# Down-projection of a hybrid decoder layer by Strassen's algorithm: seven half-size products instead of eight

## The chip, the core and the metric

The kernel runs on one core of a Trainium2 chip. The engines in this text are PE (TensorE, the matrix engine, with PEld for its weight loads), DVE (VectorE), ACT (ScalarE), POOL (GpSimd), and SP, the queue that issues most transfers. The metric is device time in microseconds (us), the median of several executions. A profile is one further execution, taken with the hardware profiler; its span runs from the first to the last instruction.

## The reference

One layer of a decoder trunk over 1024 prompt tokens and 8 sequences of 4 sample tokens, D = 1024. A mixing sub-layer comes first; then this one, in which the change lies:

```python
    h = rms_norm(x, g_ffn_pre) * (1 + sc2) + sh2
    up = h @ w_up
    up_c, new_ffn = causal_dwconv(up, past_ffn, ffn_conv_w)
    gate, val = jnp.split(up_c, 2, axis=-1)
    ff = (jax.nn.silu(gate) * val) @ w_down
    x = x + gt2 * rms_norm(ff, g_ffn_post)
```

`w_up` is 1024 x 5632 and `w_down` 2816 x 1024. All data are fp32.

## The kernel before

Every fp32 operand of a large matmul is split into a high part in fp32r (a cast on ACT) and a low part (a subtraction on DVE), and a product is three passes: high x high, low x high, high x low. A matmul takes a 128 x 128 stationary operand and streams 512 columns into one PSUM bank.

The order of the work is written by hand. `at(t, f, ...)` enters a piece of work at a virtual time, and `play()` issues all pieces in order of that time; on PE, DVE and ACT the instructions then stand in this order. SP's transfers are ordered by the compiler's scheduler. The down-projection stands behind `play()`, and there ACT and DVE are ordered by the scheduler too, only PE by the program.

**Up-projection** (`for i in range(FT)`, 22 slots). Slot i makes gate tile i and value tile i of 128 features over all tokens, by Strassen's algorithm over token halves: `prod(i, p)` (L1218) is one of seven products, 12 matmuls into one bank. Even token tiles are one half, odd ones the other. `weights` makes sums of up-weights and splits them; `c11`, `c12`, `c21`, `c22` (`comb`, L1233) add banks into the filter's input, which frees a bank; `taps2` (L1280) is the causal filter on DVE; `silu` is on ACT; and `gated` (L1290) multiplies gate and value on DVE and stores the 512 KB product tile to `ffd` in DRAM (L1293).

**Down-projection** (from L1424). Token tiles go in three groups: tiles 0 to 2, 3 to 5, 6 and 7. For each group all 22 rows of `w_down` (128 x 1024 each) are loaded and split again (`w_down(k)`: L109, L114, L119), and the activations of the group are loaded from `ffd` and split (`ff_split`: L1449, L1452, L927). `proj_k` (L723) then does, for each token tile and row, three passes into two banks, 512 columns each. psD holds four tiles of two banks, so that a group of three can be joined by the first tile of the next. The first two rows of group 0 (`first_ld`, `first_hi`, `first_lo`) are loaded and split during the up-projection. In group 1 the sample tokens are projected by `proj_s` (L727), straight from the fp32 rows. `finish` squares and sums a tile on ACT (L140), takes the power on POOL (L134), scales by the gate and adds x1 on DVE (L1472, L1473), and stores y; the last tile, 7, does so in halves (L1485 to L1534), with the last three rows kept for its end.

## Time and profile before

| | us |
|---|---|
| median of 3 runs | 1091.71 (1090.77 to 1092.13) |
| the profiled execution, its own time | 1090.5 |
| its span | 1088.7 |

| engine | busy us | share of the span |
|---|---|---|
| PE | 1058.2 | 97% |
| PEld | 888.0 | 82% |
| DVE | 773.5 | 71% |
| ACT | 468.8 | 43% |
| POOL | 29.7 | 3% |

The busy time of PE is that of pipelined instructions, so a matmul's row is longer than the time by which it sets back the next one; the distance between two starts is what counts. In a row of a group, "busy us, mean ns | idle before us <-releasers" tells how long the engine stood idle ahead of these instructions and what ended it.

### The profile page before, as it was taken

The page shows a single profiled execution, that of the slowest core. Times are in us where ns is not written, and L with a number is a line of the kernel's source. Part 1 is how long each engine was busy: PE and PEld are TensorE (multiplying, and loading weights), DVE is VectorE, ACT ScalarE, POOL GpSimd, SP SyncE. Part 2 cuts the span into 40 slices and gives each one's busy share as a digit, 9 for nine tenths or more (in the row PEclk, how much of TensorE's full clock was granted, in tenths as well). Part 3 has the DMA queues.
Part 4 walks back from the last instruction along what each step waited for, and adds up shares of the span by engine and source line. Part 5 has one row for each costly group of instructions (what it writes and reads, how often), then busy time and mean ns, then how long its engine had stood idle before and what let it go on. Part 6 is the DMA issues. An engine that isn't in the chain of part 4 may idle for free. (4 is left out here: it accounts for less than half of the span.)

```text
span 1088.7 us, 15560 instructions
## 1 busy us (share of the span) xinstructions
PE 1058.2 (97%) x6226; PEld 888.0 (82%) x6226; DVE 773.5 (71%) x1009; ACT 468.8 (43%) x797; POOL 29.7 (3%) x56
## 2 busy tenths in 40 slices
PE   5999999999999989999999999999999999999997
PEld 4999989996887768888888888888887888777786
DVE  5688898887656878778778778777776545433755
ACT  6321111124757654544544544544544434323543
POOL 3000000001011100000000000000000000000000
PEclk9999999999999999999999999999999999999999
DMA  9776651213413213122122122122125975554881
GB/s 340 256 220 195 194 193 49 61 43 95 160 43 132 88 59 117 58 78 97 58 79 97 58 78 98 58 78 97 59 73 162 327 244 166 186 192 145 283 294 49
DMA packets 54849, 145.82 MB, mean 134 GB/s; under 512 B 16628, under 2 KB 25332, under 8 KB 51704
## 3 DMA queue, kind: packets, MB, share of 16 engines
q1 hardware_dynamic: 53432, 140.49, 39.5%
q10 hardware_dynamic: 1344, 4.33, 1.0%
q8 instruction: 49, 0.80, 0.3%
q14 instruction: 24, 0.20, 0.1%
HBM read 123.55 MB, written 21.24 MB: 133 GB/s over the span
## 5 line engine op out<-in xcount | busy, mean ns | idle before, releaser
L119 DVE TENSOR_TENSOR wlo<-raw,whi 128x1024 fp32r<-128x1024 f32 x82 | 100.3, 1223 | 106.8 <-ACT whi L114 106.7
L114 ACT CAST whi<-raw 128x1024 fp32r<-128x1024 f32 x82 | 86.3, 1053 | 152.1 <-PE psd L723 116.3
L1280 DVE SCALAR_TENSOR_TENSOR facc<-fext,par,facc 128x1072 f32<-128x1072 f32 x88 | 117.2, 1332 | 14.2 <-ACT facc L1273 12.6
L535 DVE SCALAR_TENSOR_TENSOR yb<-cext,par,yb 128x1024 f32<-128x1024 f32 x90 | 111.9, 1279 | 0.8
L723 PE MATMUL psd<-whi,yhi 128*128 128x512 f32 x340 | 105.9, 391 | 0.0
L723 PE MATMUL psd<-wlo,yhi 128*128 128x512 f32 x340 | 105.4, 390 | 0.2 <-DVE ms L132 0.2
L723 PE MATMUL psd<-whi,ylo 128*128 128x512 f32 x340 | 105.3, 389 | 0.0
L279 PE MATMUL psa<-hh,whi 128*128 128x352 f32 x372 | 82.0, 328 | 0.0
L279 PE MATMUL psa<-hh,wlo 128*128 128x352 f32 x372 | 80.2, 323 | 0.0
L279 PE MATMUL psa<-hl,whi 128*128 128x352 f32 x372 | 80.1, 323 | 0.0
L723 PEld LDWEIGHTS psd<-whi,yhi 128*128 128x128 f32 x340 | 63.3, 188 | 15.3 <-issue 1.6
L723 PEld LDWEIGHTS psd<-wlo,yhi 128*128 128x128 f32 x340 | 63.7, 188 | 14.3 <-DVE wlo L119 0.6
L723 PEld LDWEIGHTS psd<-whi,ylo 128*128 128x128 f32 x340 | 63.8, 188 | 13.4
L1218 PE MATMUL psc<-hh,sh 128*128 128x512 f32 x176 | 69.3, 394 | 2.8 <-DVE fext L1233 2.8
L1218 PE MATMUL psb<-hh,sh 128*128 128x512 f32 x176 | 71.3, 405 | 0.0
L1218 PE MATMUL psc<-hl,sh 128*128 128x512 f32 x176 | 69.3, 394 | 1.2 <-DVE hl L927 1.2
L1218 PE MATMUL psc<-hh,sl 128*128 128x512 f32 x176 | 69.0, 392 | 0.0
L1218 PE MATMUL psb<-hh,sl 128*128 128x512 f32 x176 | 68.8, 391 | 0.0
L1218 PE MATMUL psc<-bh,whi 128*128 128x512 f32 x176 | 68.6, 390 | 0.0
L1218 PE MATMUL psc<-bh,wlo 128*128 128x512 f32 x176 | 68.5, 389 | 0.0
L1218 PE MATMUL psb<-hl,sh 128*128 128x512 f32 x176 | 68.5, 389 | 0.0
L1218 PE MATMUL psc<-bl,whi 128*128 128x512 f32 x176 | 68.5, 389 | 0.0
(240 smaller groups left out, 2062.3 us busy)
## 6 DMA issues: line engine op xcount, KB each, us to landing
raw<-in_w_down SPq DMA_DIRECT2D x66, 512.0 KB, 4.5
adaw<-in_ada SPq DMA_DIRECT2D x16, 1024.0 KB, 7.4
raw<-in_w_up SPq DMA_DIRECT2D x22, 512.0 KB, 3.6
rawb<-in_w_up SPq DMA_DIRECT2D x22, 512.0 KB, 3.6
ffd<-facc SPq DMA_DIRECT2D x22, 512.0 KB, 2.6
adaw<-in_adag SPq DMA_DIRECT2D x8, 1024.0 KB, 7.4
ffin<-ffd SPq DMA_DIRECT2D x42, 192.0 KB, 3.5
raw<-in_w_in SPq DMA_DIRECT2D x15, 512.0 KB, 4.2
```

The source lines that it names most:

```text
L114: act.copy(hi, ld[0])
L119: dve.tensor_tensor(out=lo, in0=ld[0], in1=hi.bitcast(F32), op=ALU.subtract)
L279: pe.matmul(ps[:, c, 0:CW], lhsT=wt[:, k, :], rhs=h[:, k, c * CW:(c + 1) * CW], start=(k == 0 and n == 0), stop=(k == KT - 1 and n == 2))
L535: dve.scalar_tensor_tensor(out=y[:, 0:NPR], in0=e[:, k:k + NPR], scalar=par[:, off + k:off + k + 1], in1=y[:, 0:NPR], op0=ALU.mult, op1=AL ...
L723: pe.matmul(ps[c], lhsT=s[:, cs], rhs=w[c], start=(first and n == 0), stop=(last and n == len(passes) - 1))
L1218: pe.matmul(out, lhsT=w[:, ks], rhs=h(k), start=(p in (1, 2, 7) and k == 0 and n == 0), stop=(k == 3 and n == 2), skip_group_check=True)
L1280: dve.scalar_tensor_tensor(out=acc[:, 0:1072], in0=e[:, k:k + 1072], scalar=par[:, wo + k:wo + k + 1], in1=acc[:, 0:1072], op0=ALU.mult, o ...
```

## The change

The product of 1024 tokens x 2816 by 2816 x 1024 is cut in halves along all three dimensions: tokens (even and odd tiles), features (even and odd 128-row blocks) and output columns (0 to 511, 512 to 1023). Seven products, each of 4 token tiles x 11 feature blocks x 512 columns, take the place of eight, in the order 2, 3, 1, 6, 5, 7, 4. A step (`step(n)`) is one feature block of one product: 12 matmuls into four banks.

- **Activation sums.** `gated` keeps an even tile's product in a buffer `g` of the pool `whi`, and `fsum` makes four sums (one after an even tile, three after an odd one). Seven half tiles of 256 KB per pair go to DRAM (`fs`), in place of two full ones.
- **Weights.** `w_down` is loaded once (`ld_row`) and stays on chip. `t_sum` makes four sums in place on DVE, three beside the steps of product 1 and one beside those of product 6.
- **Operands.** For each step `a_ld` loads one activation half tile, and `d_hi` (ACT, two casts) and `d_lo` (DVE, two subtractions) split it and the half row of weights. The first four steps are loaded and split during the up-projection.
- **Banks.** Two sets of four banks, Z and X. Products 2, 3 and 5 use Z; 1, 6, 7 and 4 use X, adding up in it. `keep` (ACT) copies Z out, `fold` (DVE) adds a bank to what has been kept. Even token tiles are finished beside product 7; the last five steps of product 4 go token tile by token tile, and each odd tile is finished as it ends.
- **Sample tokens** are projected beside product 1.
- **Order.** All of it stands in the plan of virtual times, ahead of `play()`, and SP's transfers follow that order too, from the output projection on.

```diff
-    ffd = tc.dram_tile([FT, P, NPR], F32, name="ffd")
+    fs = {p: tc.dram_tile([FT // 2, P, 512], F32, name=f"fs{p}") for p in range(1, 8)}
...
+    def tok(v):
+
+        return v[:, 0:NPR].rearrange("p (t h n) -> p t h n", h=2, n=P)
...
     def gated(i):
         ga, va = U["acc", i, 0], U["acc", i, 1]
-        dve.tensor_tensor(out=ga[:, 0:NPR], in0=ga[:, 0:NPR], in1=va[:, 0:NPR], op=ALU.mult)
+        if i % 2 == 0:
+            U["g"] = stream.tile([P, 1024], F32R, name="whi").bitcast(F32)
+            out = U["g"].rearrange("p (h t n) -> p t h n", h=2, n=P)
+        else:
+            out = tok(ga)
+        dve.tensor_tensor(out=out, in0=tok(ga), in1=tok(va), op=ALU.mult)
         dve.tensor_tensor(out=ffs[:, i].rearrange("p (s t) -> p s t", t=ST), in0=acc_parts(ga)[2],
                           in1=acc_parts(va)[2], op=ALU.mult)
-        sync.dma_start(ffd[i], ga[:, 0:NPR])
+        if i % 2 == 0:
+            sync.dma_start(fs[1][i // 2], U["g"][:, 0:512])
+        else:
+            for p, h in ((2, 0), (4, 1)):
+                sync.dma_start(fs[p][i // 2].rearrange("p (t n) -> p t n", n=P), tok(ga)[:, :, h])
+
+    def fsum(i, p):
+        g, ga, va = U["g"], U["acc", i, 0], U["acc", i, 1]
+        if p == 3:
+            sub_to(four(va[:, 0:512]), tok(ga)[:, :, 0], four(g[:, 0:512]))
+            src = va[:, 0:512]
+        elif p == 7:
+            src = va[:, 0:512]
+            sub_to(src, g[:, 0:512], g[:, 512:1024])
+        elif p == 5:
+            src = g[:, 512:1024]
+            dve.tensor_tensor(out=four(src), in0=four(src), in1=tok(ga)[:, :, 1], op=ALU.add)
+        else:
+            src = g[:, 0:512]
+            sub_to(src, g[:, 512:1024], src)
+        sync.dma_start(fs[p][i // 2], src)

...
+    FS = (6.0, 7.5, 9.0)
...
+        for n, p in enumerate((5, 6, 3) if i % 2 else (7,)):
+            at(tv + FS[n], fsum, i, p)
...
-    def first_ld(k):
-        U["wd", k] = stream.tile([P, 1024], F32, name="raw", bufs=2)
-        sync.dma_start(U["wd", k], a["w_down"][k])
-        U["ff", k] = pools["p3"].tile([P, 512], F32, name="s1", bufs=2)
-        sync.dma_start(U["ff", k][:, 0:384], ffd[k, :, 0:384])
...
-    play()
...
+    HK = FT // 2
+    PRODS = (2, 3, 1, 6, 5, 7, 4)
+    TAIL = 5
+    NP_ = len(PRODS) * HK
+    SD, SS = 2.73, 2.0
...
+    def first_b(j):
+
+        raw = stream.tile([P, 1024], F32, name="raw", bufs=2)
+        for h in range(2):
+            sync.dma_start(raw[:, 512 * h:512 * h + 512], a["w_down"][4 * j + 2 * h + 1][:, 0:512])
+        U["fb", j] = raw
...
+    def open_d():
+        psC_cm.__exit__(None, None, None)
+        psD = ctx.enter_context(tc.tile_pool(name="psD", bufs=6, space=PSUM, reuse_waits="tile"))
+        ps = [psD.tile([P, 512], F32, name="psd") for _ in range(6)]
+        W["x"], W["z"] = ps[1:3] + [psb(), psb()], ps[3:6] + ps[0:1]
+        W["s"] = W["z"][0]
...
+    def ld_row(k, hs=slice(0, D)):
+
+        if ("b", k) not in W:
+            W["b", k] = pools["p4" if k % 2 else "p5"].tile([P, D], F32, name=f"b{k}")
+        sync.dma_start(W["b", k][:, hs], a["w_down"][k][:, hs])
...
+    def t_sum(j, n):
+        e, od = W["b", 2 * j], W["b", 2 * j + 1]
+        e1, e2, o1, o2 = (v[:, 512 * h:512 * h + 512] for v in (e, od) for h in range(2))
+        sub_to(*{1: (e1, e2, e1), 3: (e2, o2, e2), 2: (o2, o2, e1), 4: (o1, o1, o2)}[n])
...
+    def a_ld(n):
+        t = R[n, "raw"] = pools["p4"].tile([P, 512], F32, name="fa", bufs=6)
+        sync.dma_start(t, fs[PRODS[n // HK]][n % HK])
...
+    def d_hi(n):
+        own = (n - 4) % 6 < 3
+        hi = (pools["p4"] if own else stream).tile([P, 1024], F32R, name="whi", **({"bufs": 3} if own else {}))
+        act.copy(hi[:, 0:512], R[n, "raw"])
+        act.copy(hi[:, 512:1024], b_raw(n))
+        R[n, "hi"] = hi
+
+    def d_lo(n):
+        own = (n - 4) % 6 < 3
+        lo, hi = (pools["p4"] if own else stream).tile([P, 1024], F32R, name="wlo", **({"bufs": 3} if own else {})), R[n, "hi"]
+        sub_to(lo[:, 0:512], R[n, "raw"], hi[:, 0:512].bitcast(F32))
+        sub_to(lo[:, 512:1024], b_raw(n), hi[:, 512:1024].bitcast(F32))
+        R[n, "a"] = hi[:, 0:512], lo[:, 0:512]
+        R[n, "b"] = hi[:, 512:1024], lo[:, 512:1024]
+
+    def step(n, pairs=range(4)):
+        p, j = PRODS[n // HK], n % HK
+        (ah, al), (bh, bl) = R[n, "a"], R[n, "b"]
+        first = j == 0 and p in (2, 3, 1, 5)
+        for t in pairs:
+            ps, cs = W["z" if p in (2, 3, 5) else "x"][t], slice(P * t, P * t + P)
+            for m, (s, w) in enumerate(((ah, bh), (al, bh), (ah, bl))):
+                pe.matmul(ps, lhsT=s[:, cs], rhs=w, start=(first and m == 0), stop=(j == HK - 1 and m == 2),
+                          skip_group_check=True)
+
+    def ymix(t, h):
+        return W["y", t][:, 512 * h:512 * h + 512]
+
+    def keep(t, p):
+        act.copy({2: lambda: ymix(t, 0), 3: lambda: ymix(t, 1), 5: lambda: W["q", t]}[p](), W["z"][t])
+
+    def fold(t, p):
+
+        out = {1: lambda: ymix(t, 0), 6: lambda: ymix(t, 1), 5: lambda: ymix(t, 1), 7: lambda: W["q", t]}[p]()
+        dve.tensor_tensor(out=out, in0=W["z" if p == 5 else "x"][t], in1=out, op=ALU.add)
+
+    def smp_rows(j):
+        for k in range(4 * j, min(4 * j + 4, FT)):
+            proj_s(W["s"], ffs[:, k, :], W["b", k], k == 0, k == FT - 1)
...
+    at(b + 0.95, open_d)
+    for n in range(4):
+        at(b + 0.96, step, n)
+    at(b + 0.97, open_4)
+    for n in range(4, NP_):
+        p, j = PRODS[n // HK], n % HK
+        at(max(b + 0.98, TS[n] - 13.0), a_ld, n)
+        if p == 2:
+            at(max(b + 0.98, TS[n] - 12.9), ld_row, 2 * j + 1)
+        if n < NP_ - TAIL:
+            at(TS[n] + 0.3, step, n)
+        first_use = min(TS[n], TS[NP_ - TAIL] + SD / 4 * (n - NP_ + TAIL))
+        lead = 6.0 if n == 4 else 7.0 if n < NP_ - TAIL else 4.5
+        for f, th in ((d_hi, first_use - lead), (d_lo, first_use - lead + 1.4)):
+            for q in (2, 3, 1, 6, 7):
+                if end(q) - 2.3 < th < end(q) + 0.1:
+                    th = end(q) + 0.1 + 0.001 * n
+            at(th, f, n)
+    for t in range(4):
+        for n in range(NP_ - TAIL, NP_):
+            at(TS[NP_ - TAIL] + SD * TAIL * t / 4, step, n, (t,))
+    for j in range(4):
+        at(TS[5 + j], ld_row, 2 * j + 1, slice(512, D))
+        at(TS[11 + j], ld_row, 2 * j + 1, slice(0, 512))
+    at(b + 18.0, open_5)
+    for j in range(HK):
+        at(TS[12] + 1.4 * SD * j, ld_row, 2 * j)
+        ts = TS[2 * HK + j]
+        for m, (n, dt) in enumerate(((1, 2.9), (3, 3.5), (2, 4.2))):
+            at(ts + dt, t_sum, j, n)
+        at(TS[3 * HK + j] - 1.0, t_sum, j, 4)
+    at(TS[3 * HK], gates2)
+    for t in range(4):
+        pt = SD / 4 * (t - 3) + 0.05
+        for p in (2, 3):
+            at(end(p) + pt, keep, t, p)
+        for p in (1, 6, 7):
+            at(end(p) + pt, fold, t, p)
+        at(end(5) + pt, keep, t, 5)
+        at(end(5) + pt + 0.5, fold, t, 5)
+        i = 2 * t
+        src = lambda t=t: W["y", t]
+        at(end(5) - 3.0 + 6.5 * t, x1_load, i)
+        at(end(5) + 3.0 + 6.5 * t, fin_sq, i, src)
+        at(end(5) + 5.0 + 6.5 * t, fin_out, i, src, "G")
+        at(end(7) + 3.0 + 3.5 * t, odd_half, t)
+        te = TS[NP_ - TAIL] + SD * TAIL * (t + 1) / 4
+        at(te - 12.0, x1_load, i + 1)
+        at(te + 0.1, odd_fin, t)
+    te = end(1) + 2.0
+    at(te - 4.0, x1_load, 8)
+    at(te, smp_f)
+    at(te + 2.0, fin_sq, 8, lambda: W["f"])
+    at(te + 8.0, fin_out, 8, lambda: W["f"], "Gs")
...
-    psD = ctx.enter_context(tc.tile_pool(name="psD", bufs=4, space=PSUM, reuse_waits="tile"))
-    pss = {}
...
```

## Rows read from the trace of the kernel before

**Rows 1.** The page's first part: busy us (share of the span), instructions.

```profile
PE 1058.2 (97%) x6226; PEld 888.0 (82%) x6226; DVE 773.5 (71%) x1009; ACT 468.8 (43%) x797; POOL 29.7 (3%) x56
```

**Rows 2.** Windows: us; PE, PEld, DVE, ACT, POOL busy; clock; DMA share; GB/s.

```profile
745.00:766.00 21.00, 21.00 (x122) 17.30 (x121) 16.17 (x23) 10.34 (x20) 0.00 (x0) 1.00 0.23 75
830.00:870.00 40.00, 39.54 (x175) 32.78 (x176) 24.45 (x30) 17.56 (x23) 0.00 (x0) 1.00 0.93 311
870.00:910.00 40.00, 40.00 (x178) 33.14 (x177) 16.34 (x19) 14.66 (x20) 0.00 (x0) 1.00 0.71 229
```

**Rows 3.** Timeline of PE at the border: start, us, operation [idle before <-releaser].

```profile
829.19 0.39 PE L1218 MATMUL psb<-hh,sl 128*128 128x512 f32 x1
830.46 0.70 PE L723 MATMUL psd<-whi,sh 128*128 128x512 f32 x2 [0.88 <-DVE fext L1233]
...
838.71 0.61 PE L723 MATMUL psd<-whi,yhi 128*128 128x512 f32 x2
...
859.56 0.62 PE L723 MATMUL psd<-whi,ylo 128*128 128x512 f32 x2
```

**Rows 4.** Timeline of PE around four sample rows.

```profile
932.57 0.61 PE L723 MATMUL psd<-wlo,yhi 128*128 128x512 f32 x2
933.12 1.93 PE L727 MATMUL psd<-raw,ffs 128*32 128x256 f32 x32
934.98 0.73 PE L723 MATMUL psd<-whi,yhi 128*128 128x512 f32 x2
```

**Rows 5.** Timeline of all engines at the end.

```profile
1082.20 0.39 PE L723 MATMUL psd<-wlo,yhi 128*128 128x512 f32 x1
...
1085.08 1.00 SPq L1534 DMA_DIRECT2D out_y<-pt  x2
```

**Rows 6.** Groups by line: count | busy us, mean ns | idle before.

```profile
L723 PE MATMUL psd<-whi,yhi 128*128 128x512 f32 x340 | 105.9, 391 | 0.0
...
L1182 ACT CAST sh<-s 128x512 fp32r<-128x512 f32 x44 | 27.3, 622 | 2.1 <-DVE s L927 2.1
...
L927 DVE TENSOR_TENSOR s<-s,raw 128x512 f32<-128x512 f32 x22 | 15.1, 684 | 0.0
L1233 DVE TENSOR_TENSOR fext<-psb,snb 128x512 f32<-128x512 f32 x22 | 15.0, 683 | 2.3 <-PE psb L1218 2.3
...
L1223 ACT COPY sna<-psc 128x512 f32<-128x512 f32 x22 | 12.8, 580 | 2.7 <-PE psc L1218 2.7
```

**Rows 7.** Timeline of DVE in a steady slot of the up-projection.

```profile
646.79 0.69 DVE L927 TENSOR_TENSOR sl<-raw,sh 128x512 fp32r<-128x512 f32 x1 [2.23 <-ACT sh L1182]
648.37 0.69 DVE L1233 TENSOR_TENSOR fext<-psc,sna 128x512 f32<-128x512 f32 x1 [0.89 <-PE psc L1218]
...
651.68 0.68 DVE L1233 TENSOR_TENSOR fext<-psb,snb 128x512 f32<-128x512 f32 x1
...
656.43 1.23 DVE L1290 TENSOR_TENSOR facc<-facc 128x1024 f32<-128x1024 f32 x1
```

**Rows 8.** Transfers from 825 to 860 us: rate in 40 slices; KB, us to landing.

```profile
GB/s 0 0 0 0 0 0 201 295 172 220 295 372 415 376 201 417 406 236 112 267 274 387 408 427 398 398 417 407 421 406 376 326 341 371 313 318 279 396 345 236
...
raw<-in_w_down SPq DMA_DIRECT2D x12, 512.0 KB, 6.3
ffin<-ffd SPq DMA_DIRECT2D x12, 192.0 KB, 5.5
```

**Rows 9.** Start of the up-projection: PE's timeline, and the window 386.4 to 389.7.

```profile
384.17 0.47 PE L1218 MATMUL psc<-hh,sh 128*128 128x512 f32 x1 [2.75 <-DVE fext L1233]
...
386.77 0.63 PE L1218 MATMUL psc<-hl,sh 128*128 128x512 f32 x1
...
389.33 0.62 PE L1218 MATMUL psc<-hl,sh 128*128 128x512 f32 x1
...
386.40:389.70 3.30, 3.30 (x9) 2.60 (x8) 2.57 (x3) 0.62 (x2) 0.30 (x2) 0.50 0.00 0
```

More of the change, by code (lines that the diff above doesn't have):

```diff
@@ L1410, in first_lo @@
-    def first_lo(k):
-        wh, yh = U["first", k]
-        wl = stream.tile([P, 1024], F32R, name="wlo")
-        sub_to(wl, U["wd", k], wh.bitcast(F32))
-        yl = pools["p3"].tile([P, 512], F32R, name="sl", bufs=5)
-        sub_to(yl[:, 0:384], U["ff", k][:, 0:384], yh[:, 0:384].bitcast(F32))
-        U["first", k] = k, (yh, yl), [halves(wh), halves(wl), U["wd", k]]
-    for k in range(2):
-        at(b - 14.0 + 5.0 * k, first_ld, k)
-        at(b - 8.0 + 3.0 * k, first_hi, k)
-        at(b - 6.9 + 3.0 * k, first_lo, k)
@@ new lines, in body, with first_b_hi @@
+    HK = FT // 2
[3 more added lines that the diff above has]
+    SD, SS = 2.73, 2.0
+    W, R = {}, {}
+    def first_b(j):
[3 more added lines that the diff above has]
+        U["fb", j] = raw
+    def first_b_hi(j):
+        hi = U["fbh", j] = stream.tile([P, 1024], F32R, name="whi")
+        act.copy(hi, U["fb", j])
@@ new lines, in first_b_lo, with first_a, first_a_hi @@
+    def first_b_lo(j):
+        lo, hi = stream.tile([P, 1024], F32R, name="wlo"), U["fbh", j]
+        sub_to(lo, U["fb", j], hi.bitcast(F32))
+        for h in range(2):
+            R[2 * j + h, "b"] = [t[:, 512 * h:512 * h + 512] for t in (hi, lo)]
+    def first_a(n):
+        raw = U["fa", n] = pools["p3"].tile([P, 512], F32, name="s1", bufs=2)
+        sync.dma_start(raw, fs[2][n])
+    def first_a_hi(n):
+        hi = U["fah", n] = pools["p3"].tile([P, 512], F32R, name="sh", bufs=5)
+        act.copy(hi, U["fa", n])
@@ new lines, in first_a_lo @@
+    def first_a_lo(n):
+        lo = pools["p3"].tile([P, 512], F32R, name="sl", bufs=5)
+        sub_to(lo, U["fa", n], U["fah", n].bitcast(F32))
+        R[n, "a"] = U["fah", n], lo
+    def open_d():
[4 more added lines that the diff above has]
+        W["s"] = W["z"][0]
@@ new lines, in gates2, with x1_load, fin_sq @@
+    def gates2():
+        W["G"] = pools["p5"].tile([P, D], F32, name="G")
+        W["Gs"] = pools["p5"].tile([NS * ST, D], F32, name="Gs")
+        load_gate(W["G"], 1)
+        load_gate_s(W["Gs"], 1)
+    def x1_load(i):
+        xt = W["xt", i] = pools["p5"].tile([P, D], F32, name="px", bufs=3)
+        sync.dma_start(xt[:tile_rows(i)], x1d[i * P:i * P + tile_rows(i), :])
+    def fin_sq(i, src):
+        rows = tile_rows(i)
+        W["r", i] = rstd_of(sq_sum(pools["p5"], src()[:rows], rows), rows, 1.0 / D)
@@ new lines, in fin_out, with smp_f @@
+    def fin_out(i, src, g):
+        rows = tile_rows(i)
+        t, xt = src(), W["xt", i]
+        dve.tensor_tensor(out=t[:rows], in0=t[:rows], in1=W[g][:rows], op=ALU.mult)
+        dve.scalar_tensor_tensor(out=t[:rows], in0=t[:rows], scalar=W["r", i][:rows], in1=xt[:rows], op0=ALU.mult, op1=ALU.add)
+        sync.dma_start(o["y"][i * P:i * P + rows], t[:rows])
+    def smp_f():
+        f = W["f"] = pools["p5"].tile([NS * ST, D], F32, name="pf")
+        for q in range(4):
+            (dve.tensor_copy, act.copy)[q % 2](f[:, 256 * q:256 * q + 256], W["s"][32 * q:32 * q + 32, 0:256])
@@ new lines, in half_sq, with odd_half @@
+    def half_sq(src):
+        junk = pools["p5"].tile([P, D], BF16, name="junk", bufs=1)
+        ss = small.tile([P, 1], F32, name="ss")
+        act.activation(junk[:, 0:512], src, AF.Square, accum_out=ss)
+        return ss
+    def odd_half(t):
+        ss = half_sq(W["q", t])
+        v0 = W["v", t] = pools["p5"].tile([P, 128], F32, name=f"v{t}")[:, 0:1]
+        dve.tensor_scalar(out=v0, in0=ss, scalar1=1.0 / D, scalar2=EPS, op0=ALU.mult, op1=ALU.add)
+        dve.tensor_tensor(out=W["q", t], in0=W["q", t], in1=W["G"][:, 512:1024], op=ALU.mult)
@@ new lines, in body @@
+    TS = {}
+    t = b + 1.0
+    for n in range(NP_):
+        if 2 * HK <= n < 3 * HK and (n - 2 * HK) % 2 == 0:
+            at(t + 0.2, smp_rows, (n - 2 * HK) // 2)
+            t += SS
+        TS[n] = t
+        t += SD
+    TS[NP_] = t
+    end = lambda p: TS[(PRODS.index(p) + 1) * HK - 1] + SD
+    for j, t0 in ((0, b - 16.0), (1, b - 12.0)):
+        at(t0, first_b, j)
+        at(t0 + (6.5 if j == 0 else 7.5), first_b_hi, j)
+        at(t0 + (7.6 if j == 0 else 8.6), first_b_lo, j)
+    for n, (t0, t1) in enumerate(((-15.9, -10.0), (-15.8, -9.0), (-8.0, -3.6), (-7.9, -2.2))):
+        at(b + t0, first_a, n)
+        at(b + t1, first_a_hi, n)
+        at(b + t1 + 0.7, first_a_lo, n)
```

145 lines of the change are left out of this document (34 added, 111 removed).

## Prediction, made before the change was run

> **What bounds the kernel now.** I read the page's engine table first: PE is busy for 97% of the span [rows 1], so a change counts if it takes matmuls away, or opens a gap between them. Then the windows: PE is full in the steady up-projection and in the down-projection, while DVE works 16.17 us of 21.00 in the first, and DMA runs at 311 GB/s just behind the border between them and at 229 GB/s later [rows 2]. Third, PE in order of time. The last up-projection matmul starts at 829.19, the first of the down-projection at 830.46 behind a wait of 0.88 us on the DVE sum that frees the bank, and then they come in pairs: from 838.71 to 859.56 there are 46 pairs in 20.85 us, 0.2266 us for each matmul [rows 3]. (The 390 ns that the groups show as the mean of one is latency; the pitch is what a matmul costs.) Every fourth weight row or so the sample tokens cut in: four rows take from 933.02 (one pair after 932.57) to 934.98, 1.96 us [rows 4]. At the end, the last matmul starts at 1082.20 and what follows is a chain through ACT, DVE and POOL to the last store [rows 5].
>
> So the down-projection holds PE from 829.42 (829.19 and one pitch) to 1082.43, that is 253.0 us. Of it 1056 matmuls (8 tiles x 22 rows x 2 halves x 3 passes; 3 x 340 in the groups [rows 6] and 36 at the start) take 239.3, the 22 sample rows 5.5 x 1.96 = 10.8, and 2.9 us are waits, 1.0 of them at the entrance.
>
> **The change, part by part.**
>
> *Matmuls.* Seven products of 11 row pairs, 4 token tiles and 3 passes are 924 matmuls of the same shape; 132 go. The up-projection's products already run twelve in a row into one bank, at the same pitch (its PE is 21.00 of 21.00 busy [rows 2]), so I take 0.2266: 924 x 0.2266 = 209.4 us. The sample rows stay, 10.8 us. The new stage is 220.2 us plus W, the waits; the old was 253.0.
>
> *Sums in the up-projection.* Per pair of tiles DVE gets four more 128x512 operations, at 0.684 each [rows 6] 2.7 us in two slots, 2.1 of them after an odd tile's product. In a slot DVE stands idle 2.23 us until ACT has cast, and later 0.89 until PE ends a product [rows 7]; it has waited for PE before it comes to the sum that PE needs next (the one at 651.68), so 2.1 us behind the product at 656.43 is absorbed. Cost nothing; without that cover it would be up to 2.1 us in each of 11 slots, 23 us. The gated product itself only writes in another order, and stays at 1.2 us (its row ends where the next begins, at 657.7).
>
> *Stores and loads.* Seven 256 KB stores per pair take the place of two of 512 KB, where the windows show 75 GB/s [rows 2]: hidden. SP follows the written order now, and waits for DVE ahead of each of these stores. What stands behind them are the next up-weights, asked for a slot ahead, and at the border the loads of steps 7 to 9. The written order also holds in the output projection, where x tiles come behind one weight row and the first up-weights behind an x tile; they are wanted by DVE and ACT later, so I take 0, and a late one costs at most its landing, 6.3 us for 512 KB [rows 8]. Three loads of w_down become one, 22 MB less; since those are hidden today, "weights on chip" gains nothing by itself.
>
> *Weight sums and operands.* A step needs four casts' worth of 128x512: two on ACT (2 x 0.622) and two subtractions on DVE (2 x 0.684) [rows 6], 1.24 and 1.37 us beside 2.72 us of PE: hidden. In the third product three weight sums come on top: DVE 5 x 0.684 = 3.4 us per step, where PE has 2.72 and on average 0.98 of sample work, 3.7. Covered, with 0.3 to spare.
>
> *The waits W.* The trace has no Strassen down-projection, so each is bounded.
> (a) Entrance: 0 if the first banks are free (the first three tiles' banks belong to finished products), 1.0 as today [rows 3]. I take 0.3.
> (b) First loads. Steps 4 to 10 each need a 256 KB activation and a 512 KB weight row, 0.79 MB in 2.72 us, 289 GB/s, and nothing of it can start before the up-projection's tiles are free at 829.4. Steps 0 to 3 give 10.9 us of cover. Today's second block is issued at the same place, and loads landed 6.3 us after issue [rows 8]. Then 1.24 on ACT and 1.37 on DVE make it some 9 us; DVE is by then through most of the last tile's sums. Step 7 is the tight one: its buffer is still being stored from, and SP asks for its data only after the last gated product. The steady slot's two filter operations, product and bank sum run from 651.68 to about 657.7 [rows 7], 6 us; with a wait for ACT and one more sum I put SP's request at 9 us: 9 + 6.3 + 2.6 = 17.9 against 19.0. Bounds 0, and 5.0 if the rate fell to the 229 GB/s of the next window (3.43 us a step, 7 x 0.71). I take 0.6, since the same window shows nine slices running between 387 and 427 GB/s [rows 8].
> (c) Bank hand-over between products. Emptying a bank takes 0.58 us on ACT or 0.69 on DVE [rows 6], and PE returns to it 2.05 us after it left. Four in a row at 0.69 against PE's 0.68 fit unless DVE is behind. Bounds 0, and 0.7 at each of four hand-overs, 2.8. I take 0.5.
> (d) The last five steps run tile by tile, so five operand pairs are wanted within 2.7 us: DVE needs 5 x 1.37 = 6.9 us from 3.1 us ahead, so the fifth is 0.8 late; 0 if DVE is early. I take 0.6.
> W is 2.0, between 0 and 9.6.
>
> *The end.* The last tile goes through the same square, mean, power, scale and two half stores [rows 5]: no change.
>
> The sum: the profiled execution has a span of 1088.7 and a time of 1090.5 us. 1090.5 - 253.0 + 220.2 + 2.0 = 1059.7. The median of the runs shown is 1091.71, 1.2 above that execution; I give part of it back and say **1060.0 us**.
>
> **A rule of the Trainium skill against it.** In 825 to 860 us DMA moved 387 to 427 GB/s over nine slices (0.9 us each) with transfers of 192 and 512 KB, several in flight [rows 8]. "DMA: Bandwidth & Descriptors", section Bandwidth, asks for transfers of 1 MiB to reach three quarters of the peak and lists 138 GB/s for 64 KB and 341 for 1 MB; for the change's 256 KB pieces I estimate some 230 GB/s from that page's two figures, and (b) would come to 7 x (0.79 MB / 230 GB/s - 2.72) = 4.8 us. The trace disagrees with it for queued transfers, by the nine slices; what it would do here is rival A.
>
> **Rivals.**
> A. *The first product waits for its loads.* For it: DMA is 93% busy in 830 to 870 today [rows 2], and SP holds the loads of steps 7 to 9 behind DVE's last sums. Against: the slices near 400 GB/s [rows 8]. Time: 1059.7 + 4.4 = 1064.
> B. *DVE becomes the bound of the third product.* Dependent sums do not overlap, and any wait on ACT adds. At 4.1 us a step instead of 3.7 it costs 11 x 0.4 = 4.4: 1064.
> C. *The up-projection's DVE queue slips*, so that a freed bank comes late to PE after every odd tile: up to 11 x 2.1 = 23 us, 1083. Against: 3.1 us of idle in every slot [rows 7], 2.23 + 0.89.
> D. *Slower than before: PE falls to its half clock.* Behind a wait of 2.75 us at 384 and a short one after it, the granted clock was 0.50 from 386.4 to 389.7, the 1.2 GHz level, and matmuls came at 0.427 us (six from 386.77 to 389.33) [rows 9]. Each matmul so run costs 0.200 more; 132 saved ones are worth 29.9 us, so 150 slow matmuls, 13 of the 77 steps, decide. If a third of the stage (308) ran so, it would be +62: 1121. For it: a wait at each of many steps, through operands made one at a time. Against: PE is fed today by the same casts and never leaves 1.00 in the stage [rows 2]. "TensorE: Matmul & The Clock Gate", section "A second HAM failure mode: psum-queue depth-cycling" in the Trainium skill, describes such a clock loss in a kernel that cycles through PSUM banks; this change cycles through four banks in a step, the trace before through three tiles with no loss.
> E. *The change does not do what it says*: as many matmuls as before. Then 1090. The diff counts 924, so this is almost nil.
>
> **How the numbers follow.** Forecast (W up to 4) 0.74, A 0.11, B 0.07, C 0.03, D 0.03, E 0.01, and 0.01 for the rest. Range: from W = 0 (1057.7), less the runs' scatter of 0.7, to W at its upper end of 9.6, 1067, where A and B lie too; it leaves out C, D and E, and a reserve for what I have not thought of. A measurement of this kernel can tell 0.2% (2.2 us) from no change. Faster by more than that: forecast, A, B, C: 0.95; within: 0.02; slower: 0.03.
>
> **What would show it.** Right: 924 matmuls in the stage besides the sample rows at a pitch of 0.227; the span from the last up-projection matmul to the last of all near 222 us; whi and subtractions on DVE waiting for PE or loads, not PE for them; PE in the steady up-projection still 21.00 busy of 21.00. A would show as PE waiting for ACT or DVE, and these for DMA, at 840 to 860; B as PE waiting for DVE subtractions around 890 to 930; C as waits on fext sums in the up-projection; D as a granted clock under 1 in the stage. I am wrong if the stage takes over 230 us, or if the up-projection grows by more than 2.

## The result, and the profile after

The changed kernel takes **1061.92 us**, the median of four executions (1059.50 to 1063.64), against 1091.92 beside it: a ratio of 0.9726, 95% interval 0.9709 to 0.9743. Run again unedited it took 1060.98 (0.9723, interval 0.9710 to 0.9737). Forecast were 1060.0, in 1057 to 1067. The profile shown here is the slowest of the first four: 1063.64, span 1061.8.

The page's first part, as in [rows 1]:

```profile
PE 1030.5 (97%) x6094; PEld 864.8 (81%) x6094; DVE 825.0 (78%) x1142; ACT 466.6 (44%) x835; POOL 38.2 (4%) x56
```

PE has 132 instructions fewer (6226 to 6094) and stays at 97%: the time went with the matmuls, and PE is still the bound. DVE has 133 more and 51.5 us more of work, in a shorter span.

The windows, with the columns of [rows 2]:

```profile
745.00:766.00 21.00, 21.00 (x122) 17.34 (x121) 16.76 (x24) 10.02 (x19) 0.00 (x0) 1.00 0.26 82
830.00:870.00 40.00, 40.00 (x178) 33.14 (x177) 30.05 (x45) 23.46 (x39) 0.00 (x0) 1.00 0.91 336
870.00:910.00 40.00, 40.00 (x247) 30.52 (x246) 21.39 (x35) 16.58 (x30) 0.00 (x0) 1.00 0.52 194
910.00:950.00 40.00, 40.00 (x234) 30.66 (x233) 34.84 (x56) 12.69 (x24) 5.67 (x1) 1.00 0.24 73
950.00:1000.00 50.00, 49.84 (x219) 40.69 (x218) 34.36 (x56) 24.39 (x45) 0.97 (x1) 1.00 0.43 129
1000.00:1040.00 40.00, 40.00 (x178) 33.14 (x177) 36.06 (x59) 22.97 (x46) 4.63 (x4) 1.00 0.63 217
272.00:277.00 5.00, 5.00 (x14) 3.63 (x15) 2.23 (x2) 4.09 (x6) 0.00 (x0) 0.66 0.00 1
```

Six things stand here. PE is full in the steady up-projection although DVE has its sums (16.76 now, 16.17 in [rows 2]). It is full at the border too, where it stood at 39.54 of 40. The clock is 1.00 all through the last stage. DMA carries 336 GB/s in its first 40 us. DVE, at 16 to 24 of 40 us in the old stage, is at 34.84 and 36.06: the next limit. And far ahead of the change, at 272 to 277 us, this execution has a granted clock of 0.66.

PE's timeline at the border, around sample rows, and at the stage's last matmul, as in [rows 3, 4, 5]:

```profile
832.00 0.39 PE L1218 MATMUL psb<-hh,sl 128*128 128x512 f32 x1
832.23 0.39 PE L1532 MATMUL psd<-whi,sh 128*128 128x512 f32 x1
...
914.42 0.39 PE L1532 MATMUL psb<-wlo,whi 128*128 128x512 f32 x1
914.74 1.93 PE L727 MATMUL psd<-b,ffs 128*32 128x256 f32 x32
916.60 0.50 PE L1532 MATMUL psd<-whi 128*128 128x512 f32 x1
...
1053.91 0.39 PE L1532 MATMUL psb<-wlo,whi 128*128 128x512 f32 x1
```

The first matmul of the stage comes one pitch behind the last of the up-projection; the 0.88 us wait of [rows 3] is gone. From 832.23 to 1053.91 are 221.7 us.

I made one table from the first and last starts of the matmul lines in each trace (us). "Middle" runs from the first matmul of the output projection (L833) to the first of the up-projection, "up-projection" from there to the first of the down-projection, "stage" from the first to the last matmul of the down-projection, "end" from there to the end of the span.

| kernel | first L833 | middle | up-projection | stage | end |
|---|---|---|---|---|---|
| before | 256.6 | 112.9 | 461.0 | 251.7 | 6.5 |
| changed | 256.3 | 115.2 | 460.8 | 221.7 | 7.9 |
| changed, again | 257.5 | 113.3 | 460.8 | 221.7 | 6.4 |

The stage gives 30.0 us in both profiles. The wait at its entrance is gone too, but the up-projection as a whole is only 0.2 us shorter for it: from the first to the last of its own matmuls (L1218) it took 459.7 us before and 460.5 in both changed profiles. The granted clock from 381 to 394 us was 0.87 in the first and 0.74 in the other two; `tail_pt` below, a changed kernel with all its sums, has 0.87 there and 459.8. So these 0.8 us go with the execution's clock and not with the sums. The first profile lost 2.3 us in the middle and 1.4 at the end; the second hardly any of either.

### The profile page after: what moved, and what is told of

The parts are those of the page before. It is cut to its first block, busy times and chain, and to the rows that moved or that the text cites. A ratio compares the mean times of both kernels' runs of the same rounds, so it can differ in the third digit from the quotient of the medians.

```text
span 1061.8 us, 15512 instructions
## 1 busy us (share of the span) xinstructions
PE 1030.5 (97%) x6094; PEld 864.8 (81%) x6094; DVE 825.0 (78%) x1142; ACT 466.6 (44%) x835; POOL 38.2 (4%) x56
## 5 line engine op out<-in xcount | busy, mean ns | idle before, releaser
L1532 PE MATMUL psd<-whi 128*128 128x512 f32 x204 | 80.1, 393 | 0.0
L1532 PE MATMUL psd<-whi,wlo 128*128 128x512 f32 x204 | 79.6, 390 | 0.1
L1532 PE MATMUL psd<-wlo,whi 128*128 128x512 f32 x204 | 79.5, 390 | 0.1
L1513 ACT CAST whi<-fa 128x512 fp32r<-128x512 f32 x73 | 45.3, 621 | 70.9 <-PE psb L1532 24.6
L927 DVE TENSOR_TENSOR wlo<-fa,whi 128x512 fp32r<-128x512 f32 x73 | 49.9, 684 | 31.0 <-ACT whi L1513 31.0
L1218 PE MATMUL psc<-hh,sh 128*128 128x512 f32 x176 | 69.7, 396 | 2.8 <-DVE fext L1233 2.8
L1218 PE MATMUL psb<-hh,sh 128*128 128x512 f32 x176 | 71.3, 405 | 0.0
L1218 PE MATMUL psc<-hl,sh 128*128 128x512 f32 x176 | 69.6, 396 | 0.9 <-DVE hl L927 0.9
L1218 PE MATMUL psc<-hh,sl 128*128 128x512 f32 x176 | 69.4, 395 | 0.0
L1218 PE MATMUL psb<-hh,sl 128*128 128x512 f32 x176 | 68.8, 391 | 0.0
L1218 PE MATMUL psc<-bh,whi 128*128 128x512 f32 x176 | 68.6, 390 | 0.0
L1218 PE MATMUL psc<-bh,wlo 128*128 128x512 f32 x176 | 68.5, 389 | 0.0
L1218 PE MATMUL psc<-bl,whi 128*128 128x512 f32 x176 | 68.5, 389 | 0.0
L1218 PE MATMUL psb<-hl,sh 128*128 128x512 f32 x176 | 68.5, 389 | 0.0
L279 PEld LDWEIGHTS psa<-hh,whi 128*128 128x128 f32 x372 | 62.8, 189 | 6.4 <-issue 4.1
L279 PEld LDWEIGHTS psa<-hh,wlo 128*128 128x128 f32 x372 | 63.8, 188 | 0.0
L279 PEld LDWEIGHTS psa<-hl,whi 128*128 128x128 f32 x372 | 63.1, 188 | 0.0
```

The lines of the kernel that those rows point to most:

```text
L279: pe.matmul(ps[:, c, 0:CW], lhsT=wt[:, k, :], rhs=h[:, k, c * CW:(c + 1) * CW], start=(k == 0 and n == 0), stop=(k == KT - 1 and n == 2))
L927: dve.tensor_tensor(out=out, in0=x, in1=y, op=ALU.subtract)
L1218: pe.matmul(out, lhsT=w[:, ks], rhs=h(k), start=(p in (1, 2, 7) and k == 0 and n == 0), stop=(k == 3 and n == 2), skip_group_check=True)
L1513: act.copy(hi[:, 0:512], R[n, "raw"])
L1532: pe.matmul(ps, lhsT=s[:, cs], rhs=w, start=(first and m == 0), stop=(j == HK - 1 and m == 2), skip_group_check=True)
```

## The experiments

**The loss ahead of the stage and the end.** Four kernels ran beside each other. `again` has no edit.

> The changed kernel once more, unedited, beside the three that follow, so that edits worth 1 to 3 us can be read against it. Theory (the profile of the changed kernel shows 1.7 us of slower matmuls after a wait at 272 us, which the other executions may or may not have): 1059.5 to 1063.6 us, as the four executions so far, and in the profile a last stage of 221 to 223 us from the first to the last matmul. Rival (the 2.8 us lost ahead of the stage belong to the change in every execution): the profile again shows the 0.5 clock behind 272 us and 1063 or more.

Measured: 1060.98 us, interval above; the profiled execution has no half clock at 272 us. PE's timeline in the changed kernel (the second row stands for those at half clock):

```profile
271.99 0.86 PE L607 MATMUL psb<-w,pw 128*128 128x352 f32 x2 [2.22 <-DVE yb L454]
...
274.62 1.38 PE L607 MATMUL psb<-w,pw 128*128 128x352 f32 x2
```

The same instruction in `again`, and then the window 272 to 277 us there:

```profile
272.53 0.86 PE L607 MATMUL psb<-w,pw 128*128 128x352 f32 x2 [1.56 <-DVE yb L454]
```

```profile
272.00:277.00 5.00, 4.47 (x19) 3.42 (x19) 2.78 (x3) 3.54 (x4) 0.00 (x0) 1.00 0.03 12
```

The wait is there in both, as before the change (1.8 us there), but only behind the wait of 2.22 us did the matmuls slow down. The eleven other profiles with this wait, the kernel before among them, have it at 1.01 to 1.81 us, a granted clock of 1.00 behind it and a middle of 112.1 to 113.8. So the middle's loss is one of the single execution. It may be part of why the eight executions of this kernel lie between 1059.2 and 1063.6.

`wlo` takes the wait away:

```diff
-    at(11.6, w_lo, 0)
+    at(14.4, w_lo, 0)
-    at(13.7, w_lo, 1)
+    at(14.5, w_lo, 1)
```

> The changed kernel with the two subtractions of w_out rows 0 and 1 moved behind the three multiplications that finish the layer norm (they stand between them on VectorE and wait for a late load there). Theory (the matmul at 272 us waits 2.2 us for a multiplication that stands behind the first subtraction, and the granted clock falls to one half behind the wait): the wait and the half clock both go, 2 to 4 us less than the unedited kernel. Rival 1 (the rows are what is late, and the wait only moves to the first matmul that uses them, at 278 us): 0 to 0.5 us less. Rival 2 (the half clock is not tied to the wait): 2.2 us less, and the half clock stays in 273 to 277 us.

Measured: 1059.22 us (1058.60 to 1062.30), ratio 0.9716, interval 0.9700 to 0.9733. The middle takes 111.4 us, where twelve profiles without this edit, the kernel before among them, have 112.1 to 115.2, and the window has neither wait nor slow matmul:

```profile
272.00:277.00 5.00, 5.00 (x22) 3.84 (x22) 0.23 (x1) 4.99 (x8) 0.00 (x0) 1.00 0.01 2
```

So the stretch is 1.9 us shorter than in `again`; in the whole time the two intervals overlap, and 1.8 us between the medians is not told apart from nothing. Rival 1 falls by the stretch. Rival 2 can't be judged: `again` had no half clock to lose.

`tail_pt` gives the end four buffers:

```diff
-        u = pools["p5"].tile([P, 512], F32, name="pt", bufs=2)
+        u = pools["p5"].tile([P, 512], F32, name="pt", bufs=4)
```

> The changed kernel with four buffers instead of two for the products of the last four odd token tiles with the gate. Theory (tile 5's product waited 2.63 us for a buffer whose store had been issued late, and so tile 5's scalings stood ahead of tile 7's): that wait is gone, from the last matmul to the end of the span 6.3 us as before the change, instead of 7.66, and 1.4 us less in the time than the unedited one. Rival (the end is set by the 5.3 us of vector work itself behind the last matmul): 7.5 us or more, and no difference.

Measured: 1059.22 us (1058.97 to 1062.22), 0.9716, interval 0.9701 to 0.9732, which overlaps that of `again`. DVE's timeline in the changed kernel:

```profile
1053.83 0.69 DVE L1593 TENSOR_TENSOR pt<-psb,G 128x512 f32<-128x512 f32 x1 [2.63 <-DMA out_y<-pt]
...
1056.64 0.15 DVE L1595 SCALAR_TENSOR_TENSOR ms<-ss,v 128x1 f32<-128x1 f32 x1
```

and in `tail_pt`:

```profile
1051.82 0.69 DVE L1593 TENSOR_TENSOR pt<-psb,G 128x512 f32<-128x512 f32 x1 [0.50 <-ACT junk L1579]
...
1055.22 0.16 DVE L1595 SCALAR_TENSOR_TENSOR ms<-ss,v 128x1 f32<-128x1 f32 x1 [0.50 <-ACT junk L1579]
```

Tile 5's product waited 2.63 us for a store to leave its buffer, and the small operation that tile 7 needs next (L1595) stood behind it on DVE until 1056.64, 2.7 us after the last matmul; with four buffers it comes 1.2 us after. The end is 6.4 us here. With two buffers it is 6.4 to 7.9 from run to run (`again`: the wait was 1.08 and the end 6.4), so the theory holds for the mechanism: the wait is gone. Its 1.4 us were the difference of one execution; what the edit is worth on average is not told apart from nothing.

`sp_auto` takes the hand-written order off SP:

```diff
-    with tc.manual_schedule(engines={mybir.EngineType.SP}):
-        play()
+    play()
```

> The changed kernel without its hand-written order for SyncE, whose issues the planner then orders as in the kernel before. Theory (the written order moved loads but none that the wait at 272 us hangs on): the wait at 272 us stays at 1.8 to 2.3 us, and the part ahead of the last stage differs by less than 1 us; in the stage itself the planner's order may bring loads late, which shows as waits of the stage's matmuls. Rival (the written order costs the 2.8 us ahead of the stage): the first matmul of the stage comes 2 to 3 us earlier, at 829.4 us as before.

Measured: **1068.45 us** (1067.26 to 1069.68), 0.9795, interval 0.9781 to 0.9809; 0.7% (7.5 us between the medians) slower than `again`, and all of it in the stage, which takes 229.2 us. The first matmul of the stage comes at 829.83, 2.4 us earlier than in the first profile, which is the sign that the rival named. But `nf_first` and `nf_wait` below keep the written order and have it at 829.85 and 829.71, with a middle of 112.9 and 113.3 (112.8 here). So the 2.4 us go with the execution, and the rival falls. The timeline of `sp_auto` (SP and PE), and then two windows of it:

```profile
829.83 0.39 PE L1532 MATMUL psd<-whi,sh 128*128 128x512 f32 x1
...
836.36 0.34 SPq L1482 DMA_DIRECT2D out_n_f<-fst  x1
...
839.61 0.40 SPq L1508 DMA_DIRECT2D fa<-fs  x1
...
845.67 0.80 PE L1532 MATMUL psd<-whi 128*128 128x512 f32 x1 [4.80 <-ACT whi L1514]
846.26 0.63 PE L1532 MATMUL psd<-whi,wlo 128*128 128x512 f32 x1
846.69 0.63 PE L1532 MATMUL psd<-wlo,whi 128*128 128x512 f32 x1
```

```profile
840.00:845.00 5.00, 0.87 (x4) 0.38 (x2) 0.69 (x1) 0.62 (x1) 0.00 (x0) 0.91 1.05 313
845.00:850.00 5.00, 4.33 (x10) 3.45 (x11) 4.35 (x7) 3.34 (x6) 0.00 (x0) 0.50 1.03 412
```

SP in the changed kernel:

```profile
832.42 0.32 SPq L1508 DMA_DIRECT2D fa<-fs  x1
832.79 0.43 SPq L1494 DMA_DIRECT2D b<-in_w_down  x1
```

This has the signs of rival A: PE waits for ACT at 845.67, and ACT for the loads. But the loads held back are those of step 4 on, not those of steps 7 to 9. The scheduler puts the store of the conv states, which waits for the last filter, and three stores of activations (two of the gated product, one of a sum) ahead of the first loads. These go out 9.8 us after the stage's first matmul (839.61 against 829.83), where the changed kernel has 0.2 (832.42 against 832.23). Step 4 waits 4.8 us, and behind the wait the granted clock is 0.50, the 1.2 GHz level: one matmul comes after 0.59 us and eleven after 0.427 instead of 0.227, another 2.6 us. 4.8 + 2.6 = 7.4 of the 7.5 us that the stage is longer.

**Is it that store?** Two kernels move it to the front by hand.

```diff
+    at(b + 0.975, n_f_out)
```

(`n_f_out` is the store, taken out of `open_5`.)

> The changed kernel with one store moved on SyncE: the 396 KB of conv states go out ahead of the first loads of step 4 instead of 18 us into the stage (the planner's order, without the hand-written one, had put it there). The store waits for the last convolution at about 836 us. Theory (that one store held all first loads back): the loads are issued 7 us later, at 839 to 840 us instead of 832.4, a matmul of step 4 or 5 waits 4 to 5 us at half clock behind it, 1067 to 1069 us, as without the written order. Rival (other loads that the planner moved were what counted): 1060 to 1062 us.

Measured: 1062.82 us (1061.17 to 1063.34), 0.9738, interval 0.9724 to 0.9753, stage 223.3. The expectation's premise was not met: at that place the store stood ahead of the last filter in the program, did not wait for it and went out at 833.68. The loads still came later, and one matmul waited 0.65 us. The timeline of `nf_first` (PE and SP):

```profile
829.85 0.39 PE L1534 MATMUL psd<-whi,sh 128*128 128x512 f32 x1
...
834.07 0.43 SPq L1510 DMA_DIRECT2D fa<-fs  x1
...
849.70 0.50 PE L1534 MATMUL psd<-whi 128*128 128x512 f32 x1 [0.65 <-ACT whi L1516]
```

The next kernel has the store in the place that was meant:

```diff
+    at(tv + 1.72, n_f_out)
-        at(max(b + 0.98, TS[n] - 13.0), a_ld, n)
+        at(max(tv + 1.75, TS[n] - 13.0), a_ld, n)
```

(and the same for `ld_row`.)

> The changed kernel with the store of the conv states put behind the operations that make the last of them, and the first loads of the last stage (steps 4 on) put behind the store; the run before this one had the store too early, so that it went out at 833.7 us, with states of the last tile that were not ready, and held nothing up. Theory (loads that stand behind this store on SyncE come 4.3 us later, at 836.7 instead of 832.4; without the written order they came 7.2 us later, and 4.8 us of that were waited for): a matmul of step 4 or 5 waits 1.5 to 2.5 us and the clock falls behind it, 2 to 5 us more than the changed kernel's 1061. Rival (the loads have so much room that 4 us more are covered): within 0.7 us.

Measured: 1066.27 us (1063.69 to 1067.25), 0.9775, interval 0.9759 to 0.9792, some 0.5% (5.3 us) over `again`; the profiled execution is the fastest of its four (1063.69). The timeline of `nf_wait` (SP and PE):

```profile
829.71 0.39 PE L1534 MATMUL psd<-whi,sh 128*128 128x512 f32 x1
...
836.23 0.34 SPq L1482 DMA_DIRECT2D out_n_f<-fst  x1
836.62 0.42 SPq L1510 DMA_DIRECT2D fa<-fs  x1
...
842.06 0.50 PE L1534 MATMUL psd<-whi 128*128 128x512 f32 x1 [1.31 <-ACT whi L1516]
...
852.07 0.50 PE L1534 MATMUL psd<-whi 128*128 128x512 f32 x1 [1.25 <-ACT whi L1516]
```

The stage takes 225.8, 4.1 more. The waits that the trace names are 1.31, at step 4, and 1.25, at step 7, and the matmuls just behind each come at up to 0.39 us (842.06, 842.39, 842.78) with a granted clock of 1.00 in the window from 840 to 845.

How late the loads are has to be counted in each execution from its own first matmul of the stage; the expectations compared times since the start of different executions, and the stage began up to 2.5 us earlier in some than in others.

| kernel | first matmul of the stage | first load issued | later than in the changed kernel | stage longer by |
|---|---|---|---|---|
| changed | 832.23 | 832.42 | 0 | 0 |
| `nf_first` | 829.85 | 834.07 | 4.0 | 1.6 |
| `nf_wait` | 829.71 | 836.62 | 6.7 | 4.1 |
| `sp_auto` | 829.83 | 839.61 | 9.6 | 7.5 |

So step 4 has some 5 us of room: in the changed kernel its last cast ends 5.0 us ahead of its first matmul, 4.0 us of lateness cost it no wait, 6.7 one of 1.31 and 9.6 one of 4.80. The tight step is 7, as the prediction had it: in `nf_first` its own load was issued only 0.5 us later (10.2 instead of 9.7 us after the stage's first matmul), but behind the late ones, its last cast ended at 19.8 instead of 16.2, and its matmul, due at 19.0, waited. The rival falls, since 4.0 us are not covered in full.

As to the question: the store of the conv states alone makes 4.1 of the 7.5 us. In `sp_auto` the three stores behind it go out from 837.61 on, 7.8 us after the stage's first matmul; in the changed kernel they go out at the same distance (from 840.00), because they wait for DVE's last products. Loads that stand behind these stores would be as late without the store of the conv states; that is argued from the issue times, and no kernel here has those three ahead of the loads without it.

**Does the same line help the kernel before?** `sp_before` has SP in written order there (the same `with` around `play()`).

> The kernel before with the one line of the change that is not Strassen: SyncE in written order up to the last stage. Theory (in the kernel before no matmul waits for a load that this order could bring earlier; the last stage shows 2.9 us of waits in all): within 1.5 us of the kernel before. Rival (the written order is worth the 7.5 us that its removal cost the changed kernel, whatever the algorithm): 1083 to 1086 us.

Measured: 1091.82 us, ratio 1.0005, interval 0.9995 to 1.0014; stage 251.7. The line is worth nothing in the output and the up-projection. It doesn't reach the old stage, which stands behind `play()`, so the run says nothing of the order there. In the changed kernel it guards the entrance of the stage, whose steps 4 to 10 need 0.79 MB each.

**Where the gain is.** `eight` issues the steps of one product twice:

```diff
             at(TS[n] + 0.3, step, n)
+            if p == 6:
+                at(TS[n] + 0.31, step, n)
```

> The changed kernel with every step of the product numbered 6 issued twice, so that the stage has 8 x 132 = 1056 matmuls again; loads, splits and stores stay as they are (that product is counted twice in what it is added to). Theory (the stage is as long as its matmuls, 226.7 ns each): 132 x 0.2267 = 29.9 us more, 251.6 us from the first to the last matmul of the stage, and 1090 to 1092 us, the time of the kernel before. Rival (the gain comes from the weights that stay on chip and from the order of the loads): 1065 to 1075 us.

Measured: 1090.12 us, ratio to the kernel before 0.9993, interval 0.9981 to 1.0005; stage 250.8, that is 29.1 more (forecast were 29.9; the changed kernel has a loss of 0.7 us at 950 us, in product 6, that `eight` hasn't). The groups of `eight` in the stage, and of the changed kernel:

```profile
L1532 PE MATMUL psd<-whi 128*128 128x512 f32 x226 | 88.6, 392 | 0.0
```

```profile
L1532 PE MATMUL psd<-whi 128*128 128x512 f32 x204 | 80.1, 393 | 0.0
```

(This is one of three passes into the banks called psd, 22 more; each pass into those called psb has 22 more too, and 6 x 22 are 132.) With as many matmuls as before, and with single loads, kept weights and SP's order all in place, the gain is gone. `onchip` is the other side, the kernel before with its weights loaded once (the later passes split a constant tile):

```diff
-        ld = split_load(a["w_down"][k], 2)
+        ld = (w0, 2) if g else split_load(a["w_down"][k], 2)
```

> The kernel before with the rows of w_down loaded in the first of its three passes over the tokens only; the other two passes split a constant tile instead, so 44 loads of 512 KB are left out, and the products of those passes are not those of the weights. Theory (weights kept on chip save nothing by themselves, since no matmul of the stage waits for such a load): within 1.5 us of the kernel before. Rival (the traffic slows the stage, and keeping weights is part of the gain): 3 us or more below.

Measured: 1091.14 us, ratio 0.9999, interval 0.9987 to 1.0011. One of its windows:

```profile
870.00:910.00 40.00, 40.00 (x178) 33.15 (x177) 16.93 (x20) 13.94 (x20) 0.00 (x0) 1.00 0.49 163
```

Traffic falls from 229 GB/s [rows 2] to 163 in this window, and PE is busy 40.00 of 40.00 us in both kernels. The rival falls.

**What the added vector work costs.** `nosums` leaves `fsum` its stores but not its sums (`src` is then the unsummed block).

> The changed kernel without the 44 sums of activation blocks in the up-projection (11 + 33 operations of 0.69 us on VectorE, 30 us); the stores stay and carry blocks that are not summed, so four of the seven products work on wrong data. Theory (the sums lie in time that VectorE has free beside the matmuls): no change, within 1.5 us of the changed kernel's 1061. Rival (VectorE's queue slips in the up-projection, as the third rival of the prediction): up to 23 us less.

Measured: 1062.36 us (1060.95 to 1063.09), 0.9735, interval 0.9721 to 0.9750; up-projection 460.7, as with them.

```profile
745.00:766.00 21.00, 21.00 (x122) 17.30 (x122) 15.69 (x22) 10.08 (x19) 0.00 (x0) 1.00 0.26 84
```

DVE has 1.07 us less in this stretch, PE the same 21.00. `dve2` goes the other way in the stage:

```diff
-        sub_to(lo[:, 512:1024], b_raw(n), hi[:, 512:1024].bitcast(F32))
+        for _ in range(2):
+            sub_to(lo[:, 512:1024], b_raw(n), hi[:, 512:1024].bitcast(F32))
```

> The changed kernel with the second of the two subtractions of every step of the last stage issued twice, 73 x 0.684 = 50 us more on VectorE. Theory (VectorE was busy 34.8 of 40 us from 910 to 950 us and 36.1 of 40 us from 1000 to 1040 us, so it has 4 to 5 us of room in each such stretch, in which 14 to 15 steps would now add 10 us): VectorE becomes the bound in those stretches, matmuls wait for it, 5 to 13 us more than the changed kernel. Rival (the splits run so far ahead that the stage carries it, 158 + 50 of 215 us): 2 us more or less.

Measured: **1080.48 us** (1080.41 to 1082.26), 0.9907, interval 0.9892 to 0.9921; 19.5 more than `again`, beyond the theory's 13. The stage takes 239.6. Windows of `dve2`, and then two rows of PE's timeline in it:

```profile
910.00:950.00 40.00, 34.51 (x196) 25.52 (x195) 37.07 (x61) 8.82 (x17) 0.03 (x1) 0.91 0.26 75
950.00:1000.00 50.00, 48.88 (x215) 39.73 (x214) 48.07 (x75) 20.71 (x38) 2.09 (x1) 1.00 0.42 129
1000.00:1040.00 40.00, 35.63 (x153) 28.81 (x152) 35.49 (x53) 19.23 (x36) 4.18 (x4) 0.97 0.41 136
```

```profile
939.16 0.77 PE L1533 MATMUL psd<-whi 128*128 128x512 f32 x1 [5.49 <-DVE ye L1545]
...
1038.62 0.77 PE L1533 MATMUL psd<-whi 128*128 128x512 f32 x1 [3.77 <-DVE yo L1545]
```

DVE falls behind within a product and PE pays where it needs a bank that DVE must empty (`fold`, here L1545): 5.5 us at the end of product 1, 3.8 at the end of product 7, 11.3 of PE's waits in all. Of the 17.9 us by which the stage is longer 6.6 are not waits that the trace names; some 5.6 of them are matmuls that come at 0.427 us behind the two long waits, where the granted clock is 0.57 from 938 to 946 us and again from 1037 to 1045. The rival (the stage as a whole has room) falls: 158 + 50 of 215 us did not fit, because the room is not where the work is.

**A version that beats both?** `best2` joins `tail_pt` and `wlo` and tries one more wait, 2.8 us at the entrance of the up-projection:

```diff
-        for dt, f in ((0, sq1), (2.2, rs), (2.4, gt), (3.7, res), (4.9, sq2), (6.0, rs), (6.8, xn2)):
+        for dt, f in ((0, sq1), (2.2, rs), (2.4, gt), (5.85, res), (5.95, sq2), (7.05, rs), (7.8, xn2)):
-        at(t8 + (6.1 if i == 0 else 14.6), c11, i)
+        at(t8 + (7.86 if i == 0 else 14.6), c11, i)
```

> The changed kernel with three edits of order: the four buffers at the end, the two subtractions of w_out rows behind the layer norm, and, at the entrance of the up-projection (383 to 390 us), the sample tile's sum and one combination behind the operations that the waiting matmul needs. Theory (these are waits of TensorE of 2.2, 2.75 and 0.9 us, with half clock behind them): the wait of 2.75 us falls to about 1.4 us, 1 to 2 us less than with the w_out edit alone, 1057 to 1058.5 us, the fastest so far. Rival (the next wait takes their place): 1059 to 1060 us.

Measured: 1059.17 us (1058.39 to 1060.21), 0.9708, interval 0.9693 to 0.9722: the smallest ratio of all, and not below `wlo` (1059.22). The rival holds. The timeline in `wlo`:

```profile
382.08 0.68 DVE L1233 TENSOR_TENSOR fext<-psc,sna 128x512 f32<-128x512 f32 x1
...
382.91 0.70 PE L1218 MATMUL psc<-hh,sh 128*128 128x512 f32 x1 [2.76 <-DVE fext L1233]
```

and in `best2`:

```profile
384.00 0.69 DVE L1233 TENSOR_TENSOR fext<-psc,sna 128x512 f32<-128x512 f32 x1
...
384.84 0.76 PE L1218 MATMUL psc<-hh,sh 128*128 128x512 f32 x1 [4.61 <-DVE fext L1233]
```

I had taken the operand `hh` for what was late, and moved the combination `c11` back to make way for it. The row names `c11` (L1233), and it was right: moved 1.92 us later, it took PE with it by 1.93, while the second wait (0.9 us, on `hl`) went. In sum that cost nothing: the granted clock from 383 to 390 us is 0.76 here and 0.51 in `wlo`, and the up-projection is 0.5 us shorter. Middle and stage are those of `wlo`. `c11` moved forward was not tried.

## Why the prediction came out right, point by point

**Matmuls.** 924 at the pitch of the old stage, 209.4 us: the stage measures 221.9 with its last pitch, forecast were 222.2. `eight` prices 132 of them at 29.1 and puts the time back on the kernel before. Rival E is out.

**The waits W** were to be 2.0; 221.9 - 209.4 - 10.8 leaves 1.7, of which none is among the four terms.
- (a) 0.3: it is 0, as the lower bound said.
- (b) 0.6: it is 0, with more room at step 7 than my 17.9 against 19.0: its last subtraction ended 17.0 us after the stage's first matmul. Step 8 was tighter, ready at 20.9 for a matmul at 22.0. My sum began with SP free to issue at the end of the up-projection, and that is so only because SP is in written order there. The text priced that order in the output projection, at 0, and not at this border. `sp_auto` shows what it guards against: 1068, where rival A had 1064 with 5.0 us of waits, for the loads of steps 7 to 9 or a slow DMA. 4.8 us were waited, but for the first loads, and the half clock behind them, 2.6, was left out; that A's size comes near is luck.
- (c) 0.5: no matmul waits for a bank at a hand-over. What the trace has is 0.9 us of weight loads that wait for DVE at 950 us, in the seventh step of product 6, 17 us behind the hand-over (PE's starts are 0.7 later for it). DVE had finished the sample tokens (L1567, L1568, from 946.88 on) ahead of that step's subtractions. W has no term for this.

```profile
948.52 1.27 DVE L1568 SCALAR_TENSOR_TENSOR pf<-pf,rs,px 32x1024 f32<-32x1024 f32 x1 [0.43 <-POOL rs L134]
950.45 0.19 PEld L1532 LDWEIGHTS psd<-whi,wlo 128*128 128x128 f32 x1 [0.48 <-DVE wlo L927]
951.05 0.19 PEld L1532 LDWEIGHTS psd<-wlo,whi 128*128 128x128 f32 x1 [0.41 <-DVE wlo L927]
```

- (d) 0.6: no wait is seen.

The other 1.0 us are in two terms that the sum took as exact. Behind the first matmul after sample rows the next one comes 0.34 us later (916.94 after 916.60) instead of 0.227, six times, 0.7 in all; and the median distance of two starts in the stage is 0.2270, not 0.2266, 0.3 over 924. Both are in the trace before as well, inside what the prediction called 2.9 us of waits. That W comes near 2.0 is thus luck in part.

**Up-projection sums** cost 0 as forecast; `nosums` gains nothing, and rival C is out.

**Product 1 on DVE** (rival B, "covered, with 0.3 to spare"): covered. `dve2` shows that the margin is real and small, as 0.684 us more in every step of the stage cost some 19.5 us. In product 1 it makes just what B priced, 6 x 0.684 = 4.1 us a step against 3.7, for which B had 4.4 us: the wait at that product's end is 5.5, and the half clock behind it, some 2.9 more, stood nowhere in B.

**"Weights on chip" and SP's order in the output projection** at 0: `onchip` and `sp_before` measure nothing clear of noise.

**Rival D.** The price of 0.200 per slow matmul holds in `sp_auto`. The stage itself ran at 1.00, with PE cycling through four banks in every step. "TensorE: Matmul & The Clock Gate" of the Trainium skill, section "A second HAM failure mode: psum-queue depth-cycling", ties the loss of clock in a kernel that cycles to short idle times of PE between groups of matmuls. Here PE was full (40.00 of 40.00 us in four windows), so the cycling alone cost no clock; the case of the page, with idle times, did not arise, and no run here tests it.

**Steps that failed.** "The end: no change": it may be up to 1.4 us longer, since tile 5's work can slip in front of tile 7's; the 6.27 I kept (6.5 in the table, less one pitch) had one tile at the end, the new stage has four in a row on two buffers. And the range began at W = 0 "less the runs' scatter of 0.7": eight executions spread over 4.4 us. The profiles put part of it in the start-up (the first L833 matmul comes between 256.2 and 258.6 us in 14 of them), part in the middle and part behind the waits at 383 us, none of which the sum had looked at. The forecast was nearer to the median than these allow one to claim, which is luck.

## To carry to other kernels

Where PE is 97% busy at full clock, count matmuls and multiply by the pitch; then find what has lost its cover. Here it was the order of one queue: stores that wait, put ahead of the first loads of a stage, took back a quarter of the gain (7.5 of 31 us), and the same line of code was worth nothing in the kernel before, where it ends ahead of the stage. Count how late a load is from the stage that needs it, not from the start of the execution. Room on an engine counts between two points where another waits for it, not over a stage. And when a wait names its releaser, move that one first (forward, I would say, which no run here shows).
